# A hybrid attention layer: queries unnormalised until the exponential, cosine product from PSUM, transposes by DMA

## The chip, the cores and the metric

The kernel runs on one core of one Trainium2 chip. The number that counts is the device time of one execution in microseconds (us). The kernel before took 2499.07 us, the median of 3 runs (2495.34 to 2501.91).

## The reference

One layer with three branches that read the same normalised input through one projection, and an output projection over all of them. The change touches branch A, grouped-query attention with per-head normalised queries and keys and rotary positions:

```python
h = rms_norm(x, norm_pre_w); proj = h @ w_in           # 2048 tokens, 1024 channels
aq = rope(rms_norm(aq.reshape(b, s, 8, 128), q_norm_w))  # 8 query heads
ak = rope(rms_norm(ak.reshape(b, s, 2, 128), k_norm_w))  # 2 key heads
p  = softmax((aq * 128 ** -0.5) @ ak.T); y_a = p @ av
# branch B: short convolution, then a bidirectional gated delta rule; branch M: attention into 256 memory tokens
out = x + rms_norm(concat(y_a, y_b, y_m) * silu(z) @ w_out, norm_post_w)
```

The rotation multiplies each head by a cosine table and adds the head with its halves swapped times a sine table. The norm of a query is one number per token and head. It can be applied to the query, or to the query's row of scores.

## The kernel before

All matrix products are made of fp16 pairs (a high part and the rest, three products each), accumulated in PSUM in fp32. The work runs in stages, one after the other on the tensor engine (PE):

- the norm of x and its transposes, and the values of branch A (up to about 117 us of the profiled span);
- the stage of queries and keys, called the **q stage** here: the tile pool `s1`, lines 417 to 483, to about 383 us;
- branch B's projections with the short convolution (pool `s2`, lines 513 to 615), called the **b stage**, to about 640 us;
- the delta rule, with projections for z and for the memory queries laid between its steps as filler (to about 1330 us);
- attention over 64 units of 256 queries and 8 memory units (to about 2155 us), and the output projection.

The q stage has 20 blocks: 4 of keys, then 4 groups of 4 blocks of queries. A block is 512 tokens by two heads. `tok_proj` issues 24 matmuls of 256 columns for 128 tokens, so 96 for a block. Two token tiles share a PSUM tile `q` of 512 columns, a **half block** in this text. The pool has four such tiles, so a fifth half block waits until the first is read. ScalarE (ACT) copies each half into `qr` with the weights' scale (line 477). `rotate` (420) then takes squares on ACT, their sums on VectorE (DVE), the sine part `t2` on GpSimd (POOL, four products, line 434), the cosine product `t1` on DVE (435), the inverse root by three Newton steps (eleven or twelve small DVE operations), the sum and the final product into `qr` (437, 438). One block later `qk_turn` (440) has PE transpose the eight 128x128 tiles of `qr` into PSUM tiles `qt`, ACT and DVE split them into the fp16 pair `qo`, and SyncE's DMA queue (SP) stores that to DRAM (`kT_d`, `qT_d`). Attention loads it from there much later, from about 1300 us on.

The tables `ct` (cosine) and `st` (sine) are loaded twice, for the keys and for the queries, and multiplied by the norm's weights (`wb`) on DVE and POOL. The names `wraw`, `wparts`, `wss`, `wc` belong to the loading and splitting of projection weights (`load_w`, 151), which runs beside everything.

The order of instructions on each engine up to the b stage is set by a scheduler that simulates the program. Each engine then runs its own list in order, and SP does so too: a DMA that waits holds up all DMAs behind it. Tiles of a later pool take the SBUF rows of an earlier one, so the b stage's first tile `xb` waits for the last readers of the q stage's tiles.

In attention a block is 128 queries against 2048 keys in two halves of 1024. `top` (1084) takes the maximum on DVE and turns it into the exponential's bias; `expo` (1101) computes the exponential on ACT with one scale `lcs` for the whole kernel; `low` (1157) turns the probabilities by transposing DMAs.

Of the kernel before, what the change touches and what calls it, by code (L numbers as in the profile page):

```python
# [25 lines left out]
EPS = 1e-6  # L26
# [11 lines left out]
def hybrid_layer(ctx: ExitStack, tc: tile.TileContext, t: dict, out, dbg=None):  # L38
# [80 lines left out]
    mkmax = const2.tile([128, 2], F32, name="mkmax")  # L119
    scales = const2.tile([128, 6], F32, name="scales")  # L120
    vs, mvs, hs_, mks, qns, kns = (scales[:, i:i + 1] for i in range(6))
    undo = const.tile([128, 21], F32, name="undo")
    vcs, mvcs, hcs, mkcs, qncs, kncs, lcs, nlcs, *gate_cs = (undo[:, i:i + 1] for i in range(16))
    mcs, lift = undo[:, 16:20], undo[:, 20:21]

    def rsqrt(pool, y, ss, shape, scale, eps, post=None):

# [72 lines left out]
    def tp_ps(name, shape=(128, 512)):  # L200
        return ps1.tile(list(shape), F32, tag="tp", name=name, bufs=4)
# [215 lines left out]
    with tc.tile_pool(name="s1", bufs=1) as p:  # L417
        pending = []

        def rotate(nm, b, qr, ct, st, post):  # L420
            sq = p.tile([128, 4, 2, 128], F32, tag="sq", name=f"sq{nm}")
            ss = p.tile([128, 8], F32, tag="ss", name=f"ss{nm}", bufs=2)
            rst = p.tile([128, 8], F32, tag="rst", name=f"rst{nm}", bufs=2)
            A.activation(sq, qr, AF.Square)
            V.tensor_reduce(ss, sq.rearrange("p a h d -> p (a h) d"), axis=AX.X, op=ALU.add)
            t1 = p.tile([128, 4, 2, 128], F32, tag="sq", name=f"t1{nm}")
            t2 = p.tile([128, 4, 2, 128], F32, tag="t2", name=f"t2{nm}")
            cb = ct[:, 4 * b:4 * b + 4, :].unsqueeze(2).to_broadcast([128, 4, 2, 128])
            for h in range(2):
                q5 = qr[:, :, h, :].rearrange("p b (a s d) -> p b a s d", a=2, s=2)  # L430
                t5 = t2[:, :, h, :].rearrange("p b (a s d) -> p b a s d", a=2, s=2)
                s5 = st[:, 4 * b:4 * b + 4, :].rearrange("p b (a s d) -> p b a s d", a=2, s=2)
                for s_ in range(2):
                    G.tensor_tensor(t5[:, :, :, s_, :], q5[:, :, :, 1 - s_, :], s5[:, :, :, s_, :], op=ALU.mult)
            V.tensor_tensor(t1, qr, cb, op=ALU.mult)
            rsqrt(p, rst, ss, [128, 8], 1.0 / 128, EPS, post)
            V.tensor_tensor(t1, t1, t2, op=ALU.add)
            V.tensor_tensor(qr, t1, rst.rearrange("p (a h) -> p a h", h=2).unsqueeze(3).to_broadcast([128, 4, 2, 128]), op=ALU.mult)

        def qk_turn(nm, b, qr, which, g):  # L440
            for h in range(2):
                pt = tp_ps(f"qt{nm}_{h}", (128, 4, 128))
                for j in range(4):
                    T.transpose(pt[:, j, :], qr[:, j, h, :], ident)
                qo = p.tile([128, 2, 4, 128], F16, tag="qo", name=f"qo{nm}_{h}", bufs=2)
                split_evac(pt, qo[:, 0], qo[:, 1])
                dst = (kT_d if which == 0 else qT_d)
                hh = h if which == 0 else 2 * g + h
                dma(dst[hh, :, :, b * 512:(b + 1) * 512], qo.rearrange("p i a b -> p i (a b)"))

        for which in range(2):
            nw = t["k_norm_w"] if which == 0 else t["q_norm_w"]
# [10 lines left out]
            norm_scale(wb.rearrange("p a d -> p (a d)"), *((kns, kncs) if which == 0 else (qns, qncs)), n=1, least=2.0 ** -45)  # L463
            V.tensor_tensor(ct, ct, wb[:, 0, :].unsqueeze(1).to_broadcast([128, TB, 128]), op=ALU.mult)
            G.tensor_tensor(st, st, wb[:, 1, :].unsqueeze(1).to_broadcast([128, TB, 128]), op=ALU.mult)
            for g in range(1 if which == 0 else 4):
                wg, (qcs,) = nxt
                for b in range(4):
                    if b == 1:
                        nxt = load_group([((which + g) * 256 if which + g < 4 else 1536, 256)])  # L470
                    nm = f"{which}_{g}_{b}"
                    qr = p.tile([128, 4, 2, 128], F32, tag="qr", name=f"qr{nm}", bufs=2)
                    for j2 in range(2):
                        ps = mm_ps(f"q{nm}_{j2}", (128, 2, 256))
                        for j in range(2):
                            tok_proj(ps[:, j, :], wg, 4 * b + 2 * j2 + j)
                        A.activation(qr[:, 2 * j2:2 * j2 + 2].rearrange("p a h d -> p a (h d)"), ps, AF.Copy, scale=qcs)
                    if pending:
                        pending.pop(0)()
                    rotate(nm, b, qr, ct, st, None if which == 0 else SCALE)  # L480
                    pending.append(lambda nm=nm, b=b, qr=qr, which=which, g=g: qk_turn(nm, b, qr, which, g))
        while pending:
            pending.pop(0)()
    V.tensor_scalar(lcs, qncs, kncs, None, op0=ALU.mult)
    V.tensor_scalar(nlcs, lcs, -1.0, None, op0=ALU.mult)
    V.tensor_scalar(lift, qns, kns, 11 * math.log(2.0), op0=ALU.mult, op1=ALU.mult)

    pin(V, Q)
    dma(tri, t["tri"])
# [196 lines left out]
    def attention_slots():  # L686
        at["v"] = slot("V", [128, 2, TB, 256], F16)
        at["PT"] = [slot(f"PT{i}", [128, 2, 2, 16, 128], F16) for i in range(2)]
        at["misc"] = wp.tile([128, D], F32, tag="whl", name="misc", bufs=4)
        V.tensor_copy(at["misc"][:, 0:128], ident)  # L690

    def load_q(nm, h, q0):
        q = zp.tile([128, 2, 2 * QW], F16, tag="th", name=f"q{nm}", bufs=3)
# [367 lines left out]
    class Block:  # L1061


        def __init__(self, u, qb):
            self.u, self.qb, self.nm = u, qb, f"{u['nm']}_{qb}"
            self.halves = []

        def score(self, k, j):
            u, nm = self.u, self.nm
# [14 lines left out]
        def top(self, k):  # L1084
            ps = self.halves[k]
            if self.u["mem"]:
                if k == 0:
                    self.mx = p.tile([128, 2, 4], F32, tag="mxm", name=f"mx{self.nm}", bufs=2)
                V.tensor_reduce(self.mx[:, k], ps.rearrange("p a (g c) -> p (a g) c", g=2), axis=AX.X, op=ALU.max, negate=True)
                for e in range(2):  # L1090
                    m = self.mx[:, k, 2 * e:2 * e + 2]
                    V.tensor_scalar(m, m, mcs[:, 2 * e:2 * e + 1], 5 * math.log(2.0), op0=ALU.mult, op1=ALU.add)
                return
            if k == 0:
                self.mx = p.tile([128, 3], F32, tag="mx", name=f"mx{self.nm}", bufs=3)
            V.tensor_reduce(self.mx[:, k:k + 1], ps.rearrange("p a c -> p (a c)"), axis=AX.X, op=ALU.max)
            if k == 1:
                V.tensor_scalar(self.mx[:, 2:3], self.mx[:, 0:1], self.mx[:, 1:2], lift, op0=ALU.max, op1=ALU.subtract)
                V.tensor_scalar(self.mx[:, 2:3], self.mx[:, 2:3], nlcs, None, op0=ALU.mult)

        def expo(self, k):
            if k == 0:
# [2 lines left out]
            if self.u["mem"]:  # L1105
# [6 lines left out]
            tb = self.tb = self.u["q0"] // 128 + self.qb  # L1112
            if k == 0:
                if tb % 8 == 0:
                    at["sm"] = p.tile([128, 8, 2], F32, tag="sm", name=f"sm{self.nm}", bufs=2)
                self.sm = at["sm"]

            A.activation(self.P[:, k], ps.rearrange("p a c -> p (a c)"), AF.Exp, bias=self.mx[:, 2:3], scale=lcs, accum_out=self.sm[:, tb % 8, k:k + 1])

        def shares(self, turn):  # L1120

# [362 lines left out]
```

## Time and profile before

| | |
|---|---|
| median of 3 runs | 2499.07 us |
| profiled execution | 2504.95 us, of which the span is 2503.2 us |
| PE busy | 2363.1 us (94% of the span) |
| DVE busy | 1694.3 us (68%) |
| ACT busy | 1282.4 us (51%) |
| POOL busy | 738.0 us (29%) |
| DMA | 452.74 MB, mean 181 GB/s |

PE is the engine that the whole kernel runs along: its share of 94% is a mean over stages, though, and in each of them the question is what PE waits for. The busy time of a matmul overlaps with the next one's, so the time per matmul is read from the starts. The granted clock of PE is 2.4 GHz nearly throughout (0.985 of it in the mean), with short stretches at 1.2 GHz.

### The profile page before, as it was taken

How to read it: one execution, taken by the hardware profiler on the slowest of the kernel's cores; microseconds unless marked ns; L12 is line 12 of the kernel's file. 1: busy time of each engine (PE TensorE's matmuls, PEld its weight loads, DVE VectorE, ACT ScalarE, POOL GpSimd, SP SyncE). 2: the span in 40 equal slices, each digit the busy share in tenths (PEclk: the TensorE clock that was granted, in tenths of full speed). 3: DMA queues.
4: the chain of work that ended last, by engine and by line, in shares of the span. 5: the costliest groups of instructions: out<-in, count | busy, mean ns of one | idle time of the engine just before them, and what ended most of it. 6: DMA issues, size and time to landing. Idle time of an engine off the chain costs nothing. (4 is left out here: it accounts for less than half of the span.)

```text
span 2503.2 us, 42751 instructions
## 1 busy us (share of the span) xinstructions
PE 2363.1 (94%) x15997; PEld 1622.6 (65%) x16005; DVE 1694.3 (68%) x3451; ACT 1282.4 (51%) x2496; POOL 738.0 (29%) x442
## 2 busy tenths in 40 slices
PE   6989999999998888999999999999999999899998
PEld 6878984555454336666664566666666667688887
DVE  7778778999758744555553777878877776355542
ACT  5533334544443134555553888888887886211110
POOL 2154431211211221121020454545556554111110
PEclk9999999999999999999999999999999999999999
DMA  6431213234388556777765999999999999674451
GB/s 222 148 99 64 81 64 77 85 110 127 108 265 235 105 154 192 225 218 217 234 207 188 215 233 246 246 236 245 238 239 240 230 226 238 197 243 155 166 169 50
DMA packets 867504, 452.74 MB, mean 181 GB/s; under 512 B 639136, under 2 KB 816864, under 8 KB 867040
## 3 DMA queue, kind: packets, MB, share of 16 engines
q1 hardware_dynamic: 854848, 407.00, 63.2%
q0 software_dynamic: 12448, 43.00, 5.0%
q8 instruction: 126, 2.06, 0.4%
q14 instruction: 82, 0.67, 0.1%
HBM read 199.20 MB, written 108.10 MB: 123 GB/s over the span
## 5 line engine op out<-in xcount | busy, mean ns | idle before, releaser
L51 PEld LDWEIGHTS <-wparts 128*128 128x128 f16 x3072 | 294.0, 98 | 325.2 <-issue 14.8
L51 POOL TENSOR_TENSOR hla<-Pa,hla 128x1281 f16<-128x1281 f32 x128 | 336.6, 2630 | 316.2 <-DVE hla L51 309.9
L51 DVE TENSOR_REDUCE mxa<-sa 128x1 f32<-128x1024 f32 x256 | 313.1, 1223 | 133.2 <-PE sa L51 132.5
L51 PE MATMUL sa<-K,qa 128*128 128x512 f16 x1536 | 375.2, 381 | 21.5 <-ACT Pa L51 19.6
L51 PE MATMUL pva<-PT,V 128*128 128x256 f16 x3072 | 377.5, 273 | 0.7 <-DVE moa L51 0.7
L51 PE MATMUL z<-hT,wparts 128*128 128x512 f16 x1536 | 373.3, 384 | 0.3
L51 PEld LDWEIGHTS <-V 128*128 128x128 f16 x3072 | 300.4, 98 | 86.9 <-issue 3.8
L51 ACT ACTIVATE Pa<-sa,mxa,undo 128x1024 f32<-128x1024 f32 x256 | 306.0, 1199 | 66.9 <-DVE mxa L51 64.1
L51 PE MATMUL o<-wo,mhl 128*128 128x512 f32 x1416 | 329.8, 395 | 11.0 <-ACT mhl L51 4.4
L51 PEld LDWEIGHTS o<-wo,mhl 128*128 128x128 f32 x1416 | 267.7, 190 | 72.6 <-ACT mhl L51 5.2
L51 ACT CAST hla<-Pa 128x2048 f16<-128x2048 f32 x128 | 243.0, 1899 | 61.2 <-DMA PT<-hla 58.3
L51 PE MATMUL b<-hT,wparts 128*128 128x512 f16 x1152 | 256.8, 379 | 0.0
L51 PEld LDWEIGHTS <-qa 128*128 128x128 f16 x1536 | 150.5, 98 | 157.8 <-issue 28.5
L51 PEld LDWEIGHTS <-hT 128*128 128x128 f16 x2304 | 226.3, 99 | 30.5 <-ACT hT L51 0.9
L51 PE MATMUL q<-wparts,hT 128*128 128x256 f16 x1920 | 216.1, 275 | 0.0
L51 POOL TENSOR_SCALAR wraw<-wraw,wsc 128x1024 f32<-128x1024 f32 (+1 forms) x22 | 67.5, 3070 | 344.4 <-DVE wy L51 267.0
L51 ACT CAST mhl<-mr 128x2048 fp32r<-128x2048 f32 (+1 forms) x16 | 29.3, 1828 | 239.2 <-PE o L51 197.3
L51 DVE SCALAR_TENSOR_TENSOR y<-xb,convw,y 128x512 f32<-128x512 f32 x192 | 149.4, 794 | 1.7
L77 POOL DMA_DIRECT2D gate<-zg x64 | 35.6, 556 | 378.0 <-DVE zg L51 205.6
L51 DVE TENSOR_TENSOR mhl<-mr,mhl 128x2048 fp32r<-128x2048 f32 (+1 forms) x16 | 60.0, 3750 | 116.0 <-ACT mhl L51 116.0
L51 POOL TENSOR_TENSOR mg<-mg 128x1536 f32<-128x1536 f32 (+1 forms) x16 | 53.5, 3343 | 260.0 <-DMA mg<-r 206.0
L51 DVE SCALAR_TENSOR_TENSOR hla<-Pa,hla 128x768 f16<-128x768 f32 x128 | 127.7, 998 | 3.1 <-ACT hla L51 1.9
(332 smaller groups left out, 3281.3 us busy)
## 6 DMA issues: line engine op xcount, KB each, us to landing
xx<-bx SPq DMA_DIRECT2D x64, 512.0 KB, 4.8
wraw<-in_w_in POOLq DMA_DIRECT2D x42, 512.0 KB, 5.5
gate<-zg POOLq DMA_DIRECT2D x64, 256.0 KB, 4.2
NI<-nit SPq DMA_DIRECT2D x32, 512.0 KB, 3.0
mr<-mix SPq DMA_DIRECT2D x13, 1024.0 KB, 5.7
mg<-r SPq DMA_DIRECT2D x13, 768.0 KB
x<-in_x SPq DMA_DIRECT2D x16, 512.0 KB, 6.5
qT<-qo SPq DMA_DIRECT2D x32, 256.0 KB, 2.9
```

The lines of the kernel that those rows point to most:

```text
L51: ins = f(*args, **kw)
L77: nc.gpsimd.dma_start(to, of)
```

## The change

Four things are changed, and the rest follows from them.

1. Queries are rotated without their norm. The sums of squares are collected per group in `qss`; `query_scales` makes the inverse roots of a whole group at once (32 columns in place of 8), times the other scales, in `qsc`. Attention reads them from a copy in `at["scale"]`: `expo` takes the scale of its own 128 queries, `top` multiplies the maximum by the negated scale and adds a constant. Keys keep their norm.
2. The cosine product reads the PSUM tile of the projection, by halves, right behind the matmuls. The copy on ACT stays, for the squares and the sine part. The PSUM tile is now free when both have read it.
3. `qk_turn` splits the rotated block into an fp16 pair `q16` before it is turned (a cast on ACT, a subtraction on DVE, 1024 columns each), and one transposing DMA on SP turns all sixteen 128x128 tiles into `qo`.
4. The stores to `kT_d` and `qT_d` read `qo` in the order in which the transposing DMA leaves it: rows of 128 fp16 values (256 bytes) instead of 512 (1024 bytes).

```diff
-        def rotate(nm, b, qr, ct, st, post):
...
-            V.tensor_tensor(t1, qr, cb, op=ALU.mult)
-            rsqrt(p, rst, ss, [128, 8], 1.0 / 128, EPS, post)
+        def rotate(nm, b, qr, t1, st, ss):
+            sq = p.tile([128, 4, 2, 128], F32, tag="sq", name=f"sq{nm}")
+            A.activation(sq, qr, AF.Square)
+            V.tensor_reduce(ss, sq, axis=AX.X, op=ALU.add)
+            t2 = turned_by(nm, b, qr, st)
+            if nm[0] == "1":
+                V.tensor_tensor(qr, t1, t2, op=ALU.add)
+                return
+            rst = p.tile([128, 8], F32, tag="rst", name=f"rst{nm}", bufs=2)
+            rsqrt(p, rst, ss.rearrange("p a h -> p (a h)"), [128, 8], 1.0 / 128, EPS)
             V.tensor_tensor(t1, t1, t2, op=ALU.add)
             V.tensor_tensor(qr, t1, rst.rearrange("p (a h) -> p a h", h=2).unsqueeze(3).to_broadcast([128, 4, 2, 128]), op=ALU.mult)
+        def query_scales(g, ss, qcs):
+            ss, y = (x[:, g].rearrange("p b h -> p (b h)") for x in (ss, qsc))
+            V.tensor_scalar(gs, qcs, 2.0 ** 26, None, op0=ALU.mult)
+            V.tensor_scalar(ss, ss, gs, gs, op0=ALU.mult, op1=ALU.mult)
+            rsqrt(p, y, ss, [128, 2 * TB], 1.0 / 128, EPS, SCALE)
+            V.tensor_scalar(y, y, gs, lcs, op0=ALU.mult, op1=ALU.mult)
         def qk_turn(nm, b, qr, which, g):
+            q16 = p.tile([128, 2, 4, 2, 128], F16, tag="q16", name=f"q16{nm}", bufs=2, align_bytes=512)
+            A.copy(q16[:, 0], qr)
+            V.tensor_tensor(q16[:, 1], qr, q16[:, 0], op=ALU.subtract)
+            qo = p.tile([128, 2, 4, 2, 128], F16, tag="qo", name=f"qo{nm}", bufs=2, align_bytes=512)
+            nc.sync.dma_start_transpose(qo.rearrange("p i b h c -> p (i b h) c"), q16.rearrange("p i b h d -> p (i b h d)"))
             for h in range(2):
-                pt = tp_ps(f"qt{nm}_{h}", (128, 4, 128))
-                for j in range(4):
-                    T.transpose(pt[:, j, :], qr[:, j, h, :], ident)
-                qo = p.tile([128, 2, 4, 128], F16, tag="qo", name=f"qo{nm}_{h}", bufs=2)
-                split_evac(pt, qo[:, 0], qo[:, 1])
-                dma(dst[hh, :, :, b * 512:(b + 1) * 512], qo.rearrange("p i a b -> p i (a b)"))
+                dma(dst[hh, :, :, b * 512:(b + 1) * 512].rearrange("d i (b c) -> d i b c", c=128), qo[:, :, :, h])
...
+                    t1 = p.tile([128, 4, 2, 128], F32, tag="t1", name=f"t1{nm}")
                     for j2 in range(2):
-                        A.activation(qr[:, 2 * j2:2 * j2 + 2].rearrange("p a h d -> p a (h d)"), ps, AF.Copy, scale=qcs)
+                        A.activation(qr[:, two], ps, AF.Copy, scale=down)
+                        V.tensor_tensor(t1[:, two], ps, cb, op=ALU.mult)
...
-                V.tensor_scalar(self.mx[:, 2:3], self.mx[:, 0:1], self.mx[:, 1:2], lift, op0=ALU.max, op1=ALU.subtract)
-                V.tensor_scalar(self.mx[:, 2:3], self.mx[:, 2:3], nlcs, None, op0=ALU.mult)
+                V.tensor_scalar(self.mx[:, 2:3], self.mx[:, 0:1], self.mx[:, 1:2], self.of(1), op0=ALU.max, op1=ALU.mult)
+                V.tensor_scalar(self.mx[:, 2:3], self.mx[:, 2:3], 11 * math.log(2.0), None, op0=ALU.add)
...
-            A.activation(self.P[:, k], ps.rearrange("p a c -> p (a c)"), AF.Exp, bias=self.mx[:, 2:3], scale=lcs, accum_out=self.sm[:, tb % 8, k:k + 1])
+            A.activation(self.P[:, k], ps.rearrange("p a c -> p (a c)"), AF.Exp, bias=self.mx[:, 2:3], scale=self.of(0), accum_out=self.sm[:, tb % 8, k:k + 1])
```

How the lists of the engines move is shown at three places. The first is PE's list in the q stage, where the keys' last block (`qt_0_3`) is turned among the matmuls of the queries' first blocks, with the small matmul `wss` of a weight load behind it. Before:

```order
L51 LDWEIGHTS hT_480
L51 MATMUL q_0_1_0_2285<-wparts,hT_480 128x256
L51 MATMUL qt_0_3_0_2210<-ident,qr_0_3_1945 128x128 x4
L51 MATMUL qt_0_3_1_2219<-ident,qr_0_3_1945 128x128 x4
L51 LDWEIGHTS onesb
L51 MATMUL wss_2270<-wsb_2265,onesb 128x1
```

After:

```order
L51 LDWEIGHTS hT_480
L51 MATMUL q_0_0_1_2138<-wparts,hT_480 128x256
L51 LDWEIGHTS onesb
L51 MATMUL wss_2219<-wsb_2214,onesb 128x1
L51 LDWEIGHTS hT_481
L51 MATMUL q_0_1_0_2235<-wparts,hT_481 128x256
```

The transposes are gone, here and at nineteen other places; `wss` has moved forward to the end of the half block before. The rest of PE's list in the q stage is the same.

The second place is SP's list in the same stage, at the keys' third block (`qo_0_2`) and the loading of the queries' tables. Before:

```order
L51 DMA kT<-qo_0_1_0_1905 256x1x512
L51 DMA kT<-qo_0_1_1_1914 256x1x512
L51 DMA st_2092<-in_sin 128x16x128
L51 DMA kT<-qo_0_2_0_2051 256x1x512
L51 DMA kT<-qo_0_2_1_2060 256x1x512
L51 DMA ct_2091<-in_cos 128x16x128
```

After:

```order
L461 DMA_TRANSPOSE qo_0_1_1899<-q_0_1_1896 128x16x128
L51 DMA kT<-qo_0_1_1899 256x4x128 x2
L461 DMA_TRANSPOSE qo_0_2_2035<-q_0_2_2032 128x16x128
L51 DMA ct_2064<-in_cos 128x16x128
L51 DMA st_2065<-in_sin 128x16x128
L51 DMA kT<-qo_0_2_2035 256x4x128 x2
```

Each pair of stores now stands behind a transposing DMA that it has to wait for, and the queries' cosine table is asked for before the sine table, ahead of the third block's stores.

The third place is DVE's list where the keys' cosine table has just been scaled and the first block is worked on (`t_0_0` is `t1`, then the sum; `ss` the squares' sums; `wparts` a weight split). Before:

```order
L51 TENSOR_TENSOR ct_1479<-ct_1479,wb_1481 128x2048
L51 TENSOR_SCALAR wc_1646<-wy_1635,undo 128x1
L51 TENSOR_REDUCE ss_0_0_1599<-sq_0_0_1598 128x8
L51 SCALAR_TENSOR_TENSOR wparts<-wraw,wsc_1637,wparts 128x1024
L51 TENSOR_TENSOR t_0_0_1603<-qr_0_0_1497,ct_1479 128x1024
L51 TENSOR_SCALAR rs_x<-ss_0_0_1599 128x8
```

After:

```order
L51 TENSOR_TENSOR ct_1480<-ct_1480,wb_1482 128x2048
L51 TENSOR_SCALAR undo<-wc_1649 128x1
L51 TENSOR_REDUCE ss_0_0_1603<-sq_0_0_1604 128x8
L51 SCALAR_TENSOR_TENSOR wparts<-wraw,wsc_1640,wparts 128x1024
L51 TENSOR_TENSOR t_0_0_1500<-q_0_0_0_1501,ct_1480 128x512
L51 TENSOR_TENSOR t_0_0_1500<-q_0_0_1_1552,ct_1480 128x512
```

The product stands at the same place, but it now reads the PSUM tiles `q_0_0_0` and `q_0_0_1`, which stay taken until it has run.

## Rows read from the trace of the kernel before

**Rows 1.** Busy time by stage (--windows): window, length, then each engine's busy time.
```profile
207.00:363.00 156.00, 156.00 (x1414) 140.26 (x1414) 120.00 (x273) 60.55 (x88) 60.68 (x64) 0.99 0.23 77
...
392.00:640.00 248.00, 247.35 (x1265) 127.31 (x1264) 241.41 (x578) 120.38 (x304) 39.84 (x23) 1.00 0.36 106
...
1330.00:2155.00 825.00, 796.26 (x5363) 534.23 (x5361) 604.56 (x897) 630.88 (x819) 389.86 (x161) 0.99 1.03 230
```

**Rows 2.** The projection's matmuls (tile q): count, ns min/median/max, first and last start.
```profile
L51 PE MATMUL q<-wparts,hT x1920: 269/273/421, 117.4 to 362.9; 128*128 128x256 f16 x192
```

**Rows 3.** What PE waited for from 110 to 400 us: total, times, longest.
```profile
PE qt L51 <- DVE qr L51: 14.2, 3, 7.4
```

**Rows 4.** PE in order of time: start, length, instruction, count, idle before.
```profile
152.52 1.97 PE L51 MATMUL qt<-ident,qr 128*128 128x128 f32 x8 [7.43 <-DVE qr L51]
154.28 10.18 PE L51 MATMUL q<-wparts,hT 128*128 128x256 f16 x81
164.30 1.04 PE L51 MATMUL qt<-ident,qr 128*128 128x128 f32 x8
...
174.78 11.85 PE L51 MATMUL q<-wparts,hT 128*128 128x256 f16 x107
...
205.65 1.97 PE L51 MATMUL qt<-ident,qr 128*128 128x128 f32 x8 [5.12 <-DVE qr L51]
207.41 11.01 PE L51 MATMUL q<-wparts,hT 128*128 128x256 f16 x82
...
366.45 12.25 PE L51 MATMUL b<-hT,wparts 128*128 128x512 f16 x56
```

**Rows 5.** DVE in order of time, the q stage's first block and the b stage's start.
```profile
132.93 2.29 DVE L51 TENSOR_TENSOR ct<-ct,wb 128x2048 f32<-128x2048 f32 x1
...
136.39 4.30 DVE L51 SCALAR_TENSOR_TENSOR wparts<-wraw,wsc,wparts 128x1024 f16<-128x1024 f32 x1
...
149.99 1.22 DVE L51 TENSOR_TENSOR t<-t,t 128x1024 f32<-128x1024 f32 x1
...
390.56 0.19 DVE L51 TENSOR_SCALAR convw<-convw 128x60 f32<-128x60 f32 x1 [1.84 <-DMA convw<-in_conv_w]
```

**Rows 6.** POOL in order of time at the first block.
```profile
132.98 6.62 POOL L51 TENSOR_TENSOR st<-st,wb 128x2048 f32<-128x2048 f32 x1 [12.00 <-DVE wsc L51]
139.59 4.87 POOL L51 TENSOR_SCALAR wraw<-wraw,wsc 128x1024 f32<-128x1024 f32 x1
144.44 2.75 POOL L51 TENSOR_TENSOR t<-qr,st 128x256 f32<-128x256 f32 x4
```

**Rows 7.** Groups of instructions from 120 to 390 us: count, busy us, mean ns, idle before.
```profile
L51 ACT ACTIVATE qr<-q,wc 128x512 f32<-128x512 f32 x40 | 27.4, 686 | 85.5 <-PE q L51 80.5 <-PE wss L51 5.0
L51 DVE TENSOR_TENSOR qo<-qt,qo 128x512 f16<-128x512 f32 x40 | 26.4, 681 | 6.4 <-ACT qo L51 6.4
...
L51 DVE TENSOR_TENSOR t<-t,t 128x1024 f32<-128x1024 f32 x20 | 24.3, 1217 | 0.1
...
L51 ACT ACTIVATE sq<-qr 128x1024 f32<-128x1024 f32 x20 | 21.1, 1054 | 19.0 <-DVE qr L51 18.7
```

**Rows 8.** The transposing DMAs of attention (tile PT): ns on SP, and landing.
```profile
L1162 SPq DMA_TRANSPOSE PT<-hla x128: 3918/4235/7255, 1384.5 to 2124.7; - x128
...
DMA to landing us min/median/max: 5.5/6.1/10.8
```

**Rows 9.** Time of a store's issue on SP (tile qo), ns min/median/max.
```profile
L51 SPq DMA_DIRECT2D qT<-qo x32: 513/513/1053, 210.0 to 381.1; - x32
```

**Rows 10.** DMA issues (--dma): count, KB each, us to landing.
```profile
qT<-qo SPq DMA_DIRECT2D x32, 256.0 KB, 2.9
...
ni<-NI SPq DMA_DIRECT2D x32, 64.0 KB, 5.3
```

**Rows 11.** ACT in order of time where the b stage's first tile is written.
```profile
383.70 2.64 ACT L51 ACTIVATE xb<-b,wc 128x512 f32<-128x512 f32 x4 [3.45 <-DMA qT<-qo]
```

**Rows 12.** The bias of attention's exponential (tile mxa), ns min/median/max.
```profile
L51 DVE TENSOR_SCALAR mxa<-mxa,undo x256: 212/244/277, 1372.9 to 2107.7; 128x1 f32<-128x1 f32 x128
```

More of the change, by code (lines that the diff above doesn't have):

```diff
@@ L121, in hybrid_layer @@
     vs, mvs, hs_, mks, qns, kns = (scales[:, i:i + 1] for i in range(6))
-    undo = const.tile([128, 21], F32, name="undo")
-    vcs, mvcs, hcs, mkcs, qncs, kncs, lcs, nlcs, *gate_cs = (undo[:, i:i + 1] for i in range(16))
-    mcs, lift = undo[:, 16:20], undo[:, 20:21]
+    undo = const.tile([128, 20], F32, name="undo")
+    vcs, mvcs, hcs, mkcs, qncs, kncs, lcs, gs, *gate_cs = (undo[:, i:i + 1] for i in range(16))
+    mcs = undo[:, 16:20]
+    qsc = const2.tile([128, 4, TB, 2], F32, name="qsc")
     def rsqrt(pool, y, ss, shape, scale, eps, post=None):
@@ L418, in hybrid_layer, with turned_by @@
         pending = []
-        def rotate(nm, b, qr, ct, st, post):
[L421 to L426, printed above, removed]
+        def turned_by(nm, b, qr, st):
             t2 = p.tile([128, 4, 2, 128], F32, tag="t2", name=f"t2{nm}")
-            cb = ct[:, 4 * b:4 * b + 4, :].unsqueeze(2).to_broadcast([128, 4, 2, 128])
             for h in range(2):
@@ L434, in rotate @@
                     G.tensor_tensor(t5[:, :, :, s_, :], q5[:, :, :, 1 - s_, :], s5[:, :, :, s_, :], op=ALU.mult)
-            V.tensor_tensor(t1, qr, cb, op=ALU.mult)
-            rsqrt(p, rst, ss, [128, 8], 1.0 / 128, EPS, post)
+            return t2
+        def rotate(nm, b, qr, t1, st, ss):
[8 more added lines that the diff above has]
+            rsqrt(p, rst, ss.rearrange("p a h -> p (a h)"), [128, 8], 1.0 / 128, EPS)
@@ L463, in hybrid_layer @@
             norm_scale(wb.rearrange("p a d -> p (a d)"), *((kns, kncs) if which == 0 else (qns, qncs)), n=1, least=2.0 ** -45)
+            if which:
+                V.tensor_scalar(lcs, qncs, kncs, None, op0=ALU.mult)
+                qss = p.tile([128, 4, TB, 2], F32, tag="qss", name="qss")
+            down = 2.0 ** -26 if which else nxt[1][0]
+            V.tensor_scalar(wb[:, 0, :], wb[:, 0, :], down, None, op0=ALU.mult)
             V.tensor_tensor(ct, ct, wb[:, 0, :].unsqueeze(1).to_broadcast([128, TB, 128]), op=ALU.mult)
@@ L472, in hybrid_layer @@
                     qr = p.tile([128, 4, 2, 128], F32, tag="qr", name=f"qr{nm}", bufs=2)
+                    t1 = p.tile([128, 4, 2, 128], F32, tag="t1", name=f"t1{nm}")
                     for j2 in range(2):
-                        ps = mm_ps(f"q{nm}_{j2}", (128, 2, 256))
+                        ps = mm_ps(f"q{nm}_{j2}", (128, 2, 2, 128))
                         for j in range(2):
-                            tok_proj(ps[:, j, :], wg, 4 * b + 2 * j2 + j)
-                        A.activation(qr[:, 2 * j2:2 * j2 + 2].rearrange("p a h d -> p a (h d)"), ps, AF.Copy, scale=qcs)
+                            tok_proj(ps[:, j].rearrange("p h d -> p (h d)"), wg, 4 * b + 2 * j2 + j)
+                        two = slice(2 * j2, 2 * j2 + 2)
+                        A.activation(qr[:, two], ps, AF.Copy, scale=down)
+                        cb = ct[:, 4 * b + 2 * j2:4 * b + 2 * j2 + 2, :].unsqueeze(2).to_broadcast([128, 2, 2, 128])
+                        V.tensor_tensor(t1[:, two], ps, cb, op=ALU.mult)
                     if pending:
                         pending.pop(0)()
-                    rotate(nm, b, qr, ct, st, None if which == 0 else SCALE)
+                    rotate(nm, b, qr, t1, st, qss[:, g, 4 * b:4 * b + 4, :] if which else p.tile([128, 4, 2], F32, tag="ss", name=f"ss{nm}", bufs=2))
                     pending.append(lambda nm=nm, b=b, qr=qr, which=which, g=g: qk_turn(nm, b, qr, which, g))
+                if which:
+                    query_scales(g, qss, qcs)
         while pending:
             pending.pop(0)()
-    V.tensor_scalar(lcs, qncs, kncs, None, op0=ALU.mult)
-    V.tensor_scalar(nlcs, lcs, -1.0, None, op0=ALU.mult)
-    V.tensor_scalar(lift, qns, kns, 11 * math.log(2.0), op0=ALU.mult, op1=ALU.mult)
     pin(V, Q)
@@ L690, in attention_slots @@
         V.tensor_copy(at["misc"][:, 0:128], ident)
+        at["scale"] = at["misc"][:, 640:896].rearrange("p (n g b h) -> p n g b h", n=2, g=4, h=2)
+        for n in range(2):
+            V.tensor_scalar(at["scale"][:, n], qsc, 1.0 - 2 * n, None, op0=ALU.mult)
     def load_q(nm, h, q0):
@@ L1066, in __init__, with of @@
             self.halves = []
+            self.tb = u["q0"] // 128 + qb
+        def of(self, minus):
+            h = self.u["h"]
+            return at["scale"][:, minus, h // 2, self.tb, h % 2:h % 2 + 1]
         def score(self, k, j):
@@ L1111, in expo @@
                 return
-            tb = self.tb = self.u["q0"] // 128 + self.qb
+            tb = self.tb
             if k == 0:
```

## The prediction

> **What bounds the kernel now.** I read the stages first. In the middle of the q stage PE is never idle: 156.00 us busy of 156, with DVE at 120, ACT at 61 and POOL at 61 [rows 1]. In the b stage PE is busy 247.35 of 248 us, and DVE 241.41, so both are nearly full [rows 1]. In attention PE has 796 of 825 us and no other engine has more than 631 [rows 1]. So the way to an earlier end is a shorter list on PE, or fewer waits of PE, and the b stage lets a gain through only if DVE begins as much earlier as PE. I then read the waits of PE in the q stage: 14.2 us, three times, all of them transposes `qt` that stand in PE's list before DVE has finished `qr` [rows 3]. Last I read PE in order of time, to see what a transposing group takes, and what the clock does behind a wait [rows 4].
>
> **What the change removes on PE.** Matmuls follow each other at (11.85 - 0.27) / 106 = 0.109 us [rows 2, 4]. So the 1920 of them need 209.7 us, while the first and the last start are 245.5 us apart [rows 2]; 35.8 us of that is something else. It comes apart like this:
> - Eight transposes take eight steps of (1.04 - 0.27) / 7 = 0.11 us, 0.88 us in all, where the clock is full; two of the 20 groups ran at half the clock, 1.76 us from their start to the next row's [rows 4]. 18 x 0.88 + 2 x 1.76 = 19.4 us.
> - The three waits, 14.2 us [rows 3].
> - The matmuls behind the two long waits begin at the lower of the clock's two levels (1.2 GHz; 2.4 GHz otherwise). 81 matmuls took (10.18 - 0.27) / 80 = 0.124 us each, 1.2 us too much; 82 took (11.01 - 0.27) / 81 = 0.133, 1.9 us too much [rows 4]. 3.1 us.
>
> The sum is 36.7 us, of which two groups (1.8 us) lie behind the last of those matmuls. That agrees with the 35.8.
>
> **What it adds on PE: waits for PSUM.** Until now a half block was free when ACT had copied it. Now the cosine product must have run too, and it needs the table and the tile `t1`, of which there is one. Four half blocks are in PSUM, each 48 x 0.109 = 5.24 us of PE.
>
> At the first block: the table is ready at 135.2, but a weight split that takes 4.30 us beside POOL stands in front, until 140.7 [rows 5]. The first half's product, priced like the subtraction that reads 512 columns of PSUM, 0.68 us [rows 7], ends at 141.4. PE wants that tile after four halves, about 139.8: a wait of 1.6 us. The second block's product needs `t1` back, so it comes behind the sum. That needs the sine products, which POOL ends at 144.44 + 2.75 = 147.2, behind the table and a weight [rows 6]; the sum ran at 149.99 to 151.2 [rows 5] and its Newton steps stay in front of it. A reduction and the last product (1.22 us each, like the sum [rows 7]) and the half's product then end at about 154.3, and PE wants that tile at 141.4 + 2 x 5.24 = 151.9: 2.4 us. With 1 us for a lower clock behind it I take 5 us; from nothing (the order on DVE turns out kinder) to the 7.4 us of today's longest wait [rows 3].
>
> At the queries' tables the same could happen: the table is loaded, then scaled (2.29 us [rows 5]) before a tile is released. Four halves are 21 us of cover, and a load as slow as the slowest landing in these rows (10.8 us [rows 8]) with scaling and some 4 us of DVE work in front makes 17. I take 1 us, between 0 and 5.
>
> In the steady blocks nothing is near PE's 10.5 us. DVE, for queries: two products of 0.68, then squares' sums, sum and subtraction at 1.22 [rows 7], 5.0 us; the Newton steps and the last product of 1.2 us are gone there. ACT: two copies of 0.69, squares and cast at 1.05 [rows 7], 3.5 us. POOL: 2.75 us [rows 6] and its weights.
>
> **SP and the transposing DMAs.** The trace has transposing DMAs of 32 tiles: 4.24 us on SP and 6.1 us to landing [rows 8]. For 16 tiles I take half the issue and the same tail, 2.1 + 1.9 = 4.0 us, at most 6.1. The stores behind it wait for that, then take 0.5 to 1.05 us each on SP [rows 9]. Together 5.0 to 8.2 us a block, under 10.5. Queued behind them on SP are the queries' tables, and later the first loads of the b stage; nobody else in the q stage reads `kT_d` or `qT_d`, except one early load of queries for attention. So the cover is PE's time per block, and it is gone if the chain takes longer than that.
>
> **The seam to the b stage.** PE can run four units of it, 24 matmuls of (12.25 - 0.38) / 55 = 0.216 us each, 20.7 us, before ACT must write `xb`, and `xb` waits for the last stores of the q stage. Today ACT writes at 383.70 [rows 11], 20.5 us after the last matmul (362.9 + 0.3 [rows 2]): just in time. After: copy 0.7, sine products 2.75 [rows 6], sum 1.2, cast 1.05, subtraction 1.2 [rows 7], transposing DMA 4.0, stores' issue 1.0, landing 2.9 [rows 10], and about 2 us of hand-overs and of scales that `query_scales` puts in front: 16.8 us. So there is no wait, with 4 us to spare. DVE starts the b stage when the convolution's weights have come, today at 390.56 [rows 5], 27.4 us after the last matmul; they stand right behind the stores on SP, and these are issued 5 us or so earlier than today relative to PE. DVE therefore gains as much as PE or a little more, and the b stage passes the gain on. Behind it PE's list is the one of before, so it arrives whole at the end. I take 0 here, from a loss of 5 to a gain of 4 us (DVE being less behind).
>
> On these stores the Trainium skill has a rule against the change: DMA: Bandwidth & Descriptors, Specifications, wants at least 512 bytes for full rate, with a read-modify-write below, and the pieces are now 256 bytes. The rows bear this out as far as they go: 64 KB in 128-byte pieces (`ni`) landed in 5.3 us, 256 KB in 1 KB pieces in 2.9 [rows 10]. That is rival 1.
>
> **Attention.** The operations are the same in number; one of the two small ones on the maximum takes a constant instead of a column. They take 212 to 277 ns [rows 12]; the change is at most 0.03 us for 128 blocks, 4 us either way, and it lies on DVE, which is not the bound. I take 0.
>
> **The sum.** 36.7 - 5 - 1 = 30.7 us. The profiled execution took 2504.95 us, so 2474; it stands 5.9 above the median of the runs, and from the median of 2499 it makes 2468.5. The bounds: 36.7 - 7.4 - 5 - 5 - 4 = 15, and 36.7 + 4 + 4 = 45 us gained.
>
> **Rivals.**
> 1. *Small pieces make the last stores late.* If a store lands in twice the 5.3 us of `ni` (1024 pieces against 512), 10.6 us, `xb` waits until 24.5 us behind the last matmul, 3.8 us too late, and PE starts again at the lower clock; the same lateness holds the b stage's loads. Some 10 us of the gain go: about 2479. For it: today's seam has nothing to spare. Against it: the landing of `ni` stands in a busier stretch.
> 2. *No change.* The b stage is as full on DVE as on PE; if DVE starts no earlier than today, PE waits there for what it won. Then 2492 to 2506. For it: 241.41 of 248 us. Against it: DVE's last work of the q stage hangs on PE, and its Newton steps are gone.
> 3. *SP becomes the bound, and it is slower.* Each block needs a transposing DMA and two stores on SP, in order, and `q16` and `qo` have two buffers each. With a landing of 10.8 us (the longest seen [rows 8]) and 2.1 us for the stores a block takes 12.9 us, 20 blocks 258 us instead of today's 245.5: about 2510. It decides from the point where a landing takes 245.5 / 20 - 2.1 = 10.2 us. Against it: the median for twice the size is 6.1.
>
> **Chances.** The forecast, 2457 to 2482, has 0.70. Rival 1 and other part losses, 2479 to 2491, 0.15. Rival 2 has 0.08, rival 3 with anything else slower 0.07. A measurement of this kernel tells about 0.3%, 7.5 us, from no change. Faster by more than that: 0.70 + 0.15 = 0.85 and a little of rival 2's upper end, 0.86; same 0.08; slower 0.06. The range for 8 in 10 runs from 2456 to 2489.
>
> **What would show it.** Right: no `qt` on PE; the q stage's matmuls 215 to 220 us from first to last start; PE waiting only near the first two key blocks, for DVE; `xb` written within 21 us of the last matmul; all later stages as long as now, some 31 us earlier. Wrong: PE waiting in each block, for DVE or through SP; a wait of PE at the b stage's fifth unit; DVE reaching the b stage no earlier; a longer attention stage.

## The result and the profile after

The changed kernel takes 2470.43 us, the median of 4 runs (2467.84 to 2472.66), beside 2497.2 us for the kernel before (4 runs, 2493.51 to 2501.91). The ratio is 0.9904, with a 95% interval of 0.9877 to 0.993. By the medians that is 26.8 us faster, by the ratio 24 (17 to 31). The forecast was 2468.5. The profiled execution took 2470.62 us, with a span of 2468.5; that of before had 2503.2, but it stood 5.9 us above the median of its first three runs, so the spans' difference of 34.7 is larger than the medians' and is not used for the total.

By stage, the kernel after: the windows answer to [rows 1] (window, length, then PE, PEld, DVE, ACT and POOL with their counts, granted clock, DMA share, GB/s).

```profile
207.00:340.00 133.00, 133.00 (x1212) 118.18 (x1211) 80.64 (x132) 55.91 (x74) 61.08 (x64) 1.00 0.60 135
392.00:610.00 218.00, 218.00 (x1121) 112.88 (x1120) 210.97 (x511) 104.09 (x251) 36.12 (x20) 1.00 0.36 105
1300.00:2120.00 820.00, 788.52 (x5333) 530.88 (x5330) 593.90 (x894) 627.74 (x812) 388.63 (x160) 0.99 1.04 230
```

PE is still full in the q and b stages. DVE in the q stage has fallen from 0.77 of the time to 0.61. The projection's matmuls and the new transposing DMA of the kernel after (count, ns min/median/max, first and last start) answer to [rows 2, 8]:

```profile
L51 PE MATMUL q<-wparts,hT x1920: 269/273/421, 113.9 to 337.6; 128*128 128x256 f16 x192
...
L461 SPq DMA_TRANSPOSE qo<-q x20: 1335/1658/4282, 152.5 to 345.2; - x20
```

From first to last start 223.7 us pass instead of 245.5, so the q stage gives 21.8 us. PE's waits between 110 and 400 us, and then PE in order of time, after; they answer to [rows 3, 4]:

```profile
PE q L51 <- DVE t L51: 8.4, 2, 4.6
```

```profile
139.42 33.28 PE L51 MATMUL q<-wparts,hT 128*128 128x256 f16 x288 [3.82 <-DVE t L51]
...
172.56 21.42 PE L51 MATMUL q<-wparts,hT 128*128 128x256 f16 x192
198.55 23.93 PE L51 MATMUL q<-wparts,hT 128*128 128x256 f16 x192 [4.57 <-DVE t L51]
...
222.35 42.08 PE L51 MATMUL q<-wparts,hT 128*128 128x256 f16 x384
...
337.68 20.88 PE L51 MATMUL b<-hT,wparts 128*128 128x512 f16 x96
```

No `qt` is left. Two waits are new, and behind each the matmuls are slower than in the steady row: (33.28 - 0.27) / 287 and (23.93 - 0.27) / 191 against 0.109 us, 1.7 and 2.8 us too much. The granted clock there is 0.53 (139.4 to 143.0 us) and 0.50 (198.5 to 202.0) of 2.4 GHz, against 1.00 from 130 to 135. Waits and clock together take 12.9 us.

What came of the gain on the way: first matmul of the q stage 3.5 us earlier (117.4, now 113.9; runs of other versions with the same work ahead began at 113.6 to 116.9, so this is taken as spread), q stage 21.8, b stage 2.5 (363.0 to 640.3, now 337.7 to 612.5; 1.8 of it the two transposing groups), delta rule 8.5, attention nothing (739.6 us in both), and the output projection took 1.6 longer; together the 34.7. The 8.5 us are not shown to be the change's: that stage took 727.3 us in the one profile of before and 717.3 to 719.1 in three traces of the changed kernel, but also 717.3 with PE's transposes put back and 711.5 with the turn alone (experiments below).

### The profile page after: what moved, and what is told of

It is laid out like the page before. It is cut to its first block, busy times and chain, and to the rows that moved or that the text cites. A ratio compares the mean times of both kernels' runs of the same rounds, so it can differ in the third digit from the quotient of the medians.

```text
span 2468.5 us, 42244 instructions
## 1 busy us (share of the span) xinstructions
PE 2341.1 (95%) x15837; PEld 1602.9 (65%) x15845; DVE 1639.5 (66%) x3305; ACT 1277.6 (52%) x2476; POOL 741.9 (30%) x442
## 4 chain that ended last, share of the span: by engine, by line
PE 35%; DMA 9%; issue 4%; ACT 2%; DVE 2%; POOL 2%; SPq 1%; ACTq 0%; DVEq 0%; POOLq 0%
PE o L51 13%; PE sa L51 8%; PE pva L51 7%; DMA PT<-hla 6%; PE z L51 3%; POOL hla L51 1%; DMA Od<-oo 1%; ACT Pa L51 1%; SPq L51 1%; PE sm L51 1%; DMA xx<-bx 1%; DVE hla L51 1%; DMA mg<-r 0%; PE o_last L51 0%; DVE mxa L51 0%
## 5 line engine op out<-in xcount | busy, mean ns | idle before, releaser
L51 PE MATMUL o<-wo,mhl 128*128 128x512 f32 x1416 | 332.4, 397 | 10.7 <-ACT mhl L51 5.2
L51 ACT ACTIVATE Pa<-sa,mxa,misc 128x1024 f32<-128x1024 f32 x256 | 305.9, 1199 | 55.2 <-DVE mxa L51 52.3
L51 POOL TENSOR_SCALAR wraw<-wraw,wsc 128x1024 f32<-128x1024 f32 (+1 forms) x22 | 76.9, 3497 | 310.6 <-DVE wy L51 234.0
L51 DVE TENSOR_TENSOR mhl<-mr,mhl 128x2048 fp32r<-128x2048 f32 (+1 forms) x16 | 51.7, 3230 | 125.8 <-ACT mhl L51 125.8
```

The source lines that it names most:

```text
L51: ins = f(*args, **kw)
```

## Experiments

Each kernel is one edit of the kernel before or after, timed beside the kernel before on the same chip. The scheduler orders the lists of each version anew, so a version can differ from its base by more than the lines of its edit.

**The changed kernel again, the turn alone, the turn left out, the turn doubled.** The first has no edit. The second is the kernel before with the new `qk_turn` alone, the third the kernel after with the old `qk_turn`. The fourth adds a second transposing DMA of the same tile:

```diff
+            qx = p.tile([128, 2, 4, 2, 128], F16, tag="qx", ...)
+            nc.sync.dma_start_transpose(qx.rearrange("p i b h c -> p (i b h) c"), q16.rearrange(...))
```

> The changed kernel once more, to see which of its differences come again. Theory: in the first run the time came from the stage of queries and keys (21.8 us from first to last of its matmuls) and from the two groups of transposes behind it (1.8 us); the 3.5 us before that stage and the 8.5 us in the delta rule belong to the profiled runs. Then 22 to 29 us faster than before, the matmuls of the q stage again 222 to 226 us from first to last start with two waits for DVE of 8 us together, and the stretch from the first z matmul to the first score 715 to 730 us. Rival: the 8.5 us of the delta rule are part of the change; then 30 us or more faster, and that stretch is again 719 us.

> The kernel before with the new qk_turn alone: DMA turns queries and keys, but the norm stays in the query and the cosine product reads SBUF. Theory: all of the gain is PE's transposes and their waits, and the cosine product from PSUM costs 13 us of it (8.4 us of waits, 4.5 us at the lower clock). Here a half block is free again when ACT has copied it, so PE waits for nothing: 32 to 38 us faster than before, 209 to 213 us from the first to the last matmul of the q stage. Rival: without the lighter DVE (no Newton steps, no last product) DVE or POOL holds PE up; then at most 20 us faster, with waits of PE in the q stage.

> The changed kernel with the old qk_turn: PE turns queries and keys again, the norm stays out of the query and the cosine product reads PSUM. Theory: 19 us of transposes come back, and PE waits for the cosine product as in the changed kernel, and here and there for qr: between 8 us slower and 7 us faster than before. Rival: the lighter DVE is what made PE's waits go, so 15 us or more of the gain stay.

> The changed kernel with every transposing DMA of queries and keys issued twice, the second into a tile that nobody reads. Theory: SP and the DMA engines have room, since a block then takes some 2 x 1.7 us of issue, 2 us of tail and 1.3 us for the stores, 7 us of PE's 10.5; the end comes within 4 us of the changed kernel. Rival: the transposing DMAs are near the bound (SP, or the DMA engines beside the weights); then 10 us or more slower than the changed kernel, with PE waiting in each block.

Measured: again 2466.11 us, ratio 0.9881 (0.9857 to 0.9906). The turn alone 2496.82, ratio 1.0017 (0.9995 to 1.0038): no gain, and my theory fell. Without the turn 2492.8, 0.9986 (0.9969 to 1.0004): no gain that can be told from zero. Doubled 2465.06, 0.9875 (0.9851 to 0.99): SP and the DMA engines have room for twice the transposing DMAs. In its trace PE waits 11.8 us near the tables, where the undoubled kernel of that session waits 8.3, and the queries' cosine table is scaled at 183.81 instead of 178.32; the time doesn't show it. Its window:

```profile
207.00:340.00 133.00, 133.00 (x1222) 119.20 (x1221) 82.83 (x128) 51.91 (x68) 54.87 (x62) 1.00 0.93 193
```

So each half of the change alone gives nothing, and both together 27 to 30 us. The turn alone is the case to explain. Its waits of PE from 110 to 400 us, then its window, and the same window before:

```profile
PE b L51 <- ACT xb L51: 16.7, 1, 16.7
PE q L51 <- ACT qr L51: 14.9, 10, 3.6
PE wss L51 <- DVE wsb L51: 4.5, 1, 4.5
PE b L51 <- ACT qr L51: 3.5, 1, 3.5
```

```profile
207.00:340.00 133.00, 118.88 (x1064) 104.64 (x1062) 118.80 (x209) 47.90 (x62) 46.63 (x53) 0.99 0.45 106
```

```profile
207.00:340.00 133.00, 133.00 (x1203) 119.47 (x1203) 102.43 (x235) 51.94 (x76) 49.81 (x53) 0.98 0.22 74
```

The transposes are gone from PE, but in steady blocks PE now waits for ACT's copy, and at the seam 16.7 us for `xb`: what was won comes back as waits. The q stage is 11.2 us shorter than before (116.8 to 351.1), the b stage 18.3 longer (354.9 to 650.5). DVE is busy 118.80 of 133 us, more than before the edit (102.43).

**Which part is the turn's partner.** The first kernel here is the turn plus the cosine product from PSUM, the queries keeping their norm. The second is the changed kernel with the product back in SBUF:

```diff
-            V.tensor_scalar(wb[:, 0, :], wb[:, 0, :], down, None, op0=ALU.mult)
...
-                        V.tensor_tensor(t1[:, two], ps, cb, op=ALU.mult)
...
+            V.tensor_tensor(t1, qr, ct[:, 4 * b:4 * b + 4, :].unsqueeze(2).to_broadcast([128, 4, 2, 128]), op=ALU.mult)
```

The third has two buffers for `t1`, `ct` and `st` and the tables scaled by quarters; the fourth lays `q16` and `qo` out as [half, head, block], so that a store has pieces of 1024 bytes.

> The kernel before with the transposing transfers and with the cosine product taken from PSUM, while the queries keep their norm on VectorE (their norm is taken here without the group's power of two). The new theory after the turn alone gained nothing: without the transposes VectorE becomes the engine that paces a query block (118.8 of 133 us busy in the window 207 to 340 us of the turn alone, against 102.4 before), because the queries' norm is still on it; so this must stay at 2488 to 2503 us, with a queries' stage of 230 us or more and VectorE over 110 us busy in that window. The rival: it was the late release of the PSUM tiles through ScalarE's queue that held TensorE (all ten waits of the turn alone name ScalarE's copy); then this gains what the whole change gains, 2464 to 2475 us.

> The changed kernel with the cosine product taken back from PSUM: it reads ScalarE's copy of the queries in SBUF, as before; the norm's move and the transposing transfers stay. The theory: the product from PSUM buys nothing here and only adds the two waits on it (8.4 us) and the lower clock behind them (4.5 us); without it TensorE waits for neither table, so 5 to 13 us faster than the changed kernel, 2453 to 2463 us. The rival: the early product is what keeps TensorE fed, and the waits for the copies (14.2 us before) return: 2470 to 2485 us.

> The changed kernel with two buffers for the cosine products, for the cosine table and for the sine table, and the tables scaled in four quarters. The theory of the second wait: the second query block's product needs the one buffer back, which hangs on the late tables; with two of each the second wait (4.6 us, and 2.8 us of lower clock) is gone, and the first (3.8 us and 1.7) stays or shrinks, since the schedule still scales all four quarters ahead of the first product: 6 to 12 us faster than the changed kernel, 2456 to 2463 us. The rival: TensorE then waits for something else in the same place (the two copies of the queries in SBUF), and it is 0 to 3 us faster.

> The changed kernel with the two halves and the four blocks of the turned tile laid out in the other order, so that a store writes pieces of 1024 bytes and not of 256; nothing else. The theory: the short pieces cost nothing that anything waits for: within 2 us of the changed kernel (2464 to 2472 us), a store still lands some 3.0 us after its issue. The rival, by the rule on short pieces (the Trainium skill, DMA: Bandwidth & Descriptors, Specifications): the stores land in about half the time, 1.5 us, and what waits for the last of them starts earlier, 1 to 5 us faster.

Measured: turn and PSUM product 2473.58, ratio 0.9924 (0.9908 to 0.994). My second theory, that the norm's removal is the one partner, fell: either part lets the turn pay. Product back in SBUF 2460.21, 0.9882 (0.9855 to 0.9909). Doubled buffers 2461.47, 0.9882 (0.986 to 0.9903); long pieces 2465.22, 0.989 (0.9871 to 0.991). By their ratios none of these three can be told from the changed kernel, whose own were 0.9904 and 0.9881.

Turn and PSUM product, waits and window:

```profile
PE q L51 <- DVE t L51: 10.9, 4, 5.2
PE b L51 <- ACT xb L51: 7.5, 1, 7.5
```

```profile
207.00:340.00 133.00, 132.99 (x1222) 119.07 (x1220) 121.43 (x248) 50.58 (x68) 58.95 (x60) 1.00 0.55 129
```

DVE is as busy as with the turn alone and PE is fed. So it isn't DVE's busy share that decides, but how many blocks it finishes in it. Between 207 and 330 us DVE did the last product of 12 blocks here, and of 10 with the turn alone. Four blocks take it 42.6 us here (from 243.03 to 285.63) and 48.5 with the turn alone (253.54 to 302.03): 10.7 and 12.1 us a block, where PE needs 10.5. DVE's groups in that stretch, first of the kernel before, then of the turn alone, then of turn and PSUM product (count, busy us, mean ns, idle before):

```profile
L51 DVE TENSOR_TENSOR rs_u<-rs_u,rs_x 128x8 f32<-128x8 f32 x33 | 5.5, 166 | 1.0
```

```profile
L51 DVE TENSOR_TENSOR rs_u<-rs_u,rs_x 128x8 f32<-128x8 f32 x30 | 16.1, 536 | 1.0
...
L51 DVE TENSOR_TENSOR q<-qr,q 128x1024 f16<-128x1024 f32 x11 | 13.9, 1261 | 10.2 <-ACT q L51 10.2
```

```profile
L51 DVE TENSOR_TENSOR q<-qr,q 128x1024 f16<-128x1024 f32 x11 | 14.0, 1268 | 2.2 <-ACT q L51 2.2
...
L51 DVE TENSOR_TENSOR rs_u<-rs_u,rs_x 128x8 f32<-128x8 f32 x35 | 10.5, 301 | 1.2
```

Two things make a block longer on DVE in the turn alone. It stands idle 10.2 us for ACT's rounding, where the PSUM product otherwise stands between (this is read from the order in the trace, not tested). And the three Newton steps stretch: an operation on eight columns took 166 ns before and 536 here. One of them, with what POOL did beside it (turn alone, order of time):

```profile
247.53 1.56 POOL L77 DMA_DIRECT2D wraw<-in_w_in  x2 [0.30 <-POOL wparts L51]
...
248.71 3.18 DVE L51 TENSOR_TENSOR rs_u<-rs_u,rs_x 128x8 f32<-128x8 f32 x1
249.11 2.75 POOL L51 TENSOR_TENSOR t<-qr,st 128x256 f32<-128x256 f32 x4
251.93 0.17 DVE L51 SCALAR_TENSOR_TENSOR rst<-rs_u,rst 128x8 f32<-128x8 f32 x1
```

It ends when POOL's four products end. It also begins 0.40 us ahead of them, while POOL is still issuing two DMAs; why it doesn't go first isn't shown.

The version with doubled buffers shows the same thing. Its DVE and POOL, then PE, in order of time (the view ends at 160 us; POOL's fourth product ends at 162.17, DVE's two rows at 162.25):

```profile
156.13 6.12 DVE L51 TENSOR_SCALAR wb<-wb 128x128 f32<-128x128 f32 x1
156.26 5.99 DVE L51 TENSOR_TENSOR rs_u<-rs_u,rs_x 128x8 f32<-128x8 f32 x1
157.24 3.71 POOL L51 TENSOR_TENSOR st<-st,wb 128x512 f32<-128x512 f32 x3
```

```profile
141.00 22.80 PE L51 MATMUL q<-wparts,hT 128*128 128x256 f16 x192 [3.57 <-DVE t L51]
169.49 11.90 PE L51 MATMUL q<-wparts,hT 128*128 128x256 f16 x96 [5.69 <-DVE t L51]
```

The second wait at the queries' tables is gone, as expected, but POOL now scales the second sine table among the key blocks, an eight-column step on DVE stands still beside it, DVE then scales the second cosine table, and PE waits there instead, 5.69 us. This trace is of the slowest of its six runs (2471.43 us), so it doesn't show what made the median lower. With long pieces a store landed 2.5 us after its issue instead of 3.0, but pieces of 1024 bytes took 2.9 in the kernel before and pieces of 256 took 2.7 with the turn doubled. So a price of short pieces isn't shown, and no wait of PE ends on these stores.

**What holds the turn alone.** A third buffer for `qr` (`bufs=3`), and, apart from it, half the sine products:

```diff
-            for h in range(2):
+            for h in range(1):
                 q5 = qr[:, :, h, :]...
-            V.tensor_tensor(t1, t1, t2, op=ALU.add)
+            V.tensor_tensor(t1, t1, t2[:, :, 0:1, :].to_broadcast([128, 4, 2, 128]), op=ALU.add)
```

> The turn alone, with three buffers for the queries' copy in SBUF in place of two. After the third failure of a theory, two are left for the ten waits of the turn alone. First: VectorE's own period (in the window 207 to 340 us it is busy 118.8 of 133 us and waits 10.2 us for ScalarE's rounding, while it works off ten blocks: some 13 us a block, against 10.6 us of matmuls). Then a third buffer changes nothing: 2488 to 2502 us, waits of TensorE for the copies of 10 us or more in all. Second: the hand-back of a buffer, since the copy that empties a PSUM tile needs the buffer that the block two before it still holds until its rounding is done. Then the third buffer takes the waits away: 2463 to 2478 us.

> The turn alone, with two of the four sine products of each block left out on GpSimd (the second head takes the first head's). The theory: VectorE's small steps stretch while GpSimd's products run (the 8-wide product of the square root took 536 ns in the turn alone and 166 ns before, one step 3.18 us, ending with GpSimd's products), and that makes its period long; with half of the products the steps come near 200 to 300 ns, the period falls by 1 to 2 us a block and the waits for the copies from 14.9 us to under 6: 2472 to 2486 us. The rival: the products have nothing to do with it; 2488 to 2502 us and steps as long as before.

> The same kernel as in the run with the cosine product back in SBUF, beside the changed kernel on one chip. The theory: its stage of queries and keys is 5 to 6 us shorter in the traces (217.9 us from first to last matmul against 223.5), so it is 3 to 9 us faster than the changed kernel beside it. The rival: what it gains is given back in the later stages, and the two are within 2 us.

> The changed kernel once more, as the yardstick of the other three: 2464 to 2472 us, ratio to the kernel before 0.986 to 0.991.

Measured: a third buffer 2498.22, ratio 1.0009 (0.9994 to 1.0023), so `qr`'s buffers are not what is short. Half the sine products 2482.27, 0.9942 (0.9922 to 0.9963). Waits and a group of each, the third buffer first:

```profile
PE q L51 <- ACT qr L51: 12.4, 7, 3.6
...
L51 DVE TENSOR_TENSOR rs_u<-rs_u,rs_x 128x8 f32<-128x8 f32 x30 | 16.1, 535 | 1.0
```

```profile
PE b L51 <- ACT xb L51: 14.8, 1, 14.8
PE q L51 <- ACT qr L51: 3.2, 3, 2.2
...
L51 DVE TENSOR_TENSOR rs_u<-rs_u,rs_x 128x8 f32<-128x8 f32 x33 | 11.3, 342 | 1.1
```

Nothing was taken from DVE's list in the second, only from POOL's. Two of the three kinds of Newton step became shorter on DVE (342 instead of 536 ns, 167 instead of 311; the third kept its 0.31 us), four blocks take it 44.6 us (from 241.27 to 285.87), 11.1 a block instead of 12.1, and PE's waits in the blocks went from 14.9 to 3.2 us. The idle time for ACT's rounding stayed (9.5 us). The sine part is also ready sooner in it, so the two effects aren't fully apart. The seam keeps 14.8 us: 11.1 is still more than PE's 10.5, so DVE falls behind, and its last final product begins 28 us after the last matmul does (332.1 and 360.45; 31 us in the turn alone, 351.1 and 382.44).

The product back in SBUF took 2458.24 (2456.22 to 2462.76), ratio 0.9854 (0.9829 to 0.988), the changed kernel beside it 2468.68 (2460.7 to 2472.15), 0.9887 (0.9863 to 0.9912). By the medians it is the fastest version, 10.4 us ahead, a little more than the 3 to 9 expected; the two intervals still overlap. Matmuls of its q stage, and PE's waits from 110 to 400 us:

```profile
L51 PE MATMUL q<-wparts,hT x1920: 269/273/421, 116.4 to 334.1; 128*128 128x256 f16 x192
```

```profile
PE wss L51 <- DVE wsb L51: 5.5, 1, 5.5
PE bs L51 <- DVE sv L51: 0.9, 1, 0.9
```

217.7 us instead of 222.8 (114.0 to 336.8) beside it: both waits for the tables are gone, and one for a weight's scale has come. That is 5.1 of the 9.1 us between the two traces. The q stage also begins 2.4 us later in this version, and its delta rule is 7.3 us shorter (711.8 against 719.1), which the edit isn't shown to cause.

## Why the prediction was right, and which step was not

*The forecast's case came true*: 26.8, 29.5 and 26.6 us by the medians of three sessions, against 30.6 from 2499.07 to 2468.5. No rival did. By its terms the gain is smaller: 36.7 - 5.5 - 7.4 = 23.8 us, and the q and b stages gave 21.8 + 2.5 = 24.3. What makes up the rest isn't shown, so that the time came within 2 us of the forecast is in part luck. Two of the prediction's own signs failed: the q stage took 223.7 us instead of 215 to 220, and PE waited not only near the first key blocks but, longer, at the queries' tables.

*What PE loses.* Right: no transposes, the three waits gone, and so are the two last groups, which lay in the b stage.

*What PE gets: the waits for PSUM.* Forecast 5 us at the first key blocks and 1 us at the queries' tables; measured 5.5 (3.82 and 1.7 of clock) and 7.4 (4.57 and 2.8). The mis-sized term is the second one, above even its bound of 5. These are its rows, after, in order of time:

```profile
171.06 0.74 SPq L51 DMA_DIRECT2D ct<-in_cos  x1
...
172.26 1.35 SPq L51 DMA_DIRECT2D st<-in_sin  x1
...
177.40 2.29 DVE L51 TENSOR_TENSOR ct<-ct,wb 128x2048 f32<-128x2048 f32 x1 [1.77 <-DMA ct<-in_cos]
...
182.14 4.79 POOL L51 TENSOR_TENSOR st<-st,wb 128x2048 f32<-128x2048 f32 x1 [10.53 <-DMA st<-in_sin]
...
186.92 4.86 POOL L51 TENSOR_SCALAR wraw<-wraw,wsc 128x1024 f32<-128x1024 f32 x1
...
191.76 2.78 POOL L51 TENSOR_TENSOR t<-qr,st 128x256 f32<-128x256 f32 x4
191.81 1.05 ACT L51 CAST wparts<-wraw 128x1024 f16<-128x1024 f32 x1 [1.95 <-POOL wraw L51]
...
193.39 1.06 ACT L51 ACTIVATE sq<-qr 128x1024 f32<-128x1024 f32 x1
194.47 1.22 DVE L51 TENSOR_REDUCE qss<-sq 128x8 f32<-128x1024 f32 x1 [5.33 <-ACT sq L51]
194.51 2.11 POOL L51 TENSOR_TENSOR wparts<-wraw,wparts 128x1024 f16<-128x1024 f32 x1
195.61 2.09 DVE L51 TENSOR_TENSOR qr<-t,t 128x1024 f32<-128x1024 f32 x1
```

I priced the way from the cosine table to the first product, and that was in time: its table was scaled by 179.7. But the second block's product needs `t1` back, so it stands behind the first block's sum, and that hangs on the other table: `st` landed at 182.1, then POOL scaled it and, until 191.8, a weight. From there two ways lead to the sum. One is the sine products, done at 194.5. The other ends a little later: ACT rounds that weight before it copies the second block's other half and squares the block, and DVE's reduction of these squares, which stands in front of the sum, waits 5.33 us for them and ends at 195.7. The sum then takes 2.09 us beside POOL's next product instead of 1.22. The next product ended at 198.5; PE had stopped at 172.56 + 21.42 = 194.0. At the keys' tables I had followed this chain through `t1`, here I left it out.

The size at the first block was right, its course was not: one wait came instead of two, and the first was put too low, since 117.4 + 4 x 5.24 is 138.4 and not 139.8, so its 1.6 us should have been 3.0. Besides, DVE's and POOL's scaling of the two tables shifted by 0.2 us against each other. Before, DVE began first and POOL's 6.62 us hold DVE's 2.29 [rows 5, 6]. After, POOL began first (DVE's and POOL's rows of after):

```profile
129.85 6.53 DVE L51 TENSOR_TENSOR ct<-ct,wb 128x2048 f32<-128x2048 f32 x1
```

```profile
129.71 4.51 POOL L51 TENSOR_TENSOR st<-st,wb 128x2048 f32<-128x2048 f32 x1 [26.79 <-DVE wy L51]
```

134.22, POOL's end, plus 2.29 is 136.5, where DVE's row ends (136.4). The first product began at 138.68, instead of some 4 us earlier, and PE's first wait is 3.82. Such an exclusive hold for a whole instruction is what the Trainium skill says of a DVE operation with two SBUF inputs beside a GpSimd one (SBUF — State Buffer, SBUF: two separate sides), and the one that starts first is not held. For this pair the traces agree: in all thirteen that scale whole tables, the row that begins second takes 6.5 to 6.6 us. For the eight-column steps they agree on the hold alone: these began before GpSimd's products and were held all the same.

*The steady blocks.* "Nothing is near PE's 10.5 us" was right for this kernel, for a reason I had not weighed: the turn alone shows that without parts 1 and 2 DVE would have taken 12.1 us a block. (The 13 of the expectation above divides by ten blocks a window that holds eleven.) Either part is enough to bring DVE to PE's pace or close to it: 10.7 us with the PSUM product. The prediction counted the transposes' 36.7 us as the turn's gain; they are the joint gain. Part 2 was not needed beside part 1: without the PSUM product the ratio was 0.9882 and 0.9854, against 0.9881 to 0.9904 with it, and both waits at the tables were gone.

*SP and the transposing DMAs.* Forecast 2.1 us of issue and 4.0 to landing; measured 1.66 and 3.7. Doubling them cost no time: rival 3 is out.

*The seam, and short pieces.* Rows of after: the stores on SP, then ACT's `xb`; they answer to [rows 9, 11].

```profile
L51 SPq DMA_DIRECT2D qT<-qo x32: 586/630/1552, 204.4 to 349.5; - x32
```

```profile
352.73 1.85 ACT L51 ACTIVATE xb<-b,wc 128x512 f32<-128x512 f32 x3 [8.81 <-DMA tri<-in_tri]
```

14.9 us behind the last matmul, where 16.8 were forecast and 20.7 are free: PE runs on without a wait. (The row names the load of `tri`, issued right behind the last store; that store, issued at 349.5, would land 3.0 us later at 352.5, so the two can't be told apart.) A store landed in 3.0 us, against 2.9 before [rows 10], so rival 1 is out. DVE took up the convolution's weights at 358.7, 20.8 us behind the last matmul instead of 27.4: rival 2 is out.

*Attention.* The two small operations on the maximum, one group before [rows 12], are now two of 128, of 273 and of 153 ns, and the stage kept its 739.6 us. Right.

## What to carry to other kernels

Work taken from the bounding engine pays only down to the period of the next one: before counting it, write down that engine's period per block in the new order, idle time and stretched steps included (here DVE: 12.1 us in the turn alone against PE's 10.5). Where a product reads PSUM directly, follow every tile that it needs, its output buffer too, back to its slowest source; here the buffer hung on a table that the product itself never reads. A small operation on DVE can take as long as a large one where GpSimd works beside it (3.18 and 5.99 us here).

## What the runs showed of the hardware

One step of eight columns on DVE took 166 ns in the kernel before on average, and 3.18 or 5.99 us in two rows that ended with GpSimd's products on SBUF; both had begun ahead of these products. A row of 2.29 us became 6.53 beside GpSimd's scaling of the other table. In that pair the row that began second was the long one in all thirteen traces, with 0.05 us between the two before and 0.14 after. Products of 512 columns that read PSUM took 673 to 694 ns in four traces. Twenty more transposing DMAs of sixteen tiles raised the DMA share in the q stage from 0.60 to 0.93 and cost no time.
